# A gate projection by seven block products, with the residual brought back by feature tile

## The chip, the cores and the metric

The kernel runs on one core of one Trainium2 chip. The metric is the device time of that core in microseconds, the median of several runs. The profile shows one execution, with times in microseconds from the first instruction. Its engines are TensorE (PE; its weight loads apart as PEld), VectorE (DVE), ScalarE (ACT), GpSimd (POOL) and SyncE (SP), which here only issues DMAs.

## The reference

One decoder layer over 1024 tokens with 1024 features in float32. What the change touches is the last line, the gated per-layer input embedding; the half FFN before it (2816 hidden features) has the code that the change reuses:

```
x = x + 0.5 * swiglu(rms_norm(x, ffn2_norm), w_gate, w_up, w_down)
x = x + sigmoid(rms_norm(x, ple_norm) @ w_ple_gate) * (p @ w_ple_proj)
```

`w_ple_gate` is 1024 x 1024; `p @ w_ple_proj` is computed at the start of the kernel and lies in DRAM (`pd`, eight tiles of 128 features by 1024 tokens).

## The kernel before, in words

Activations lie with features on the 128 partitions and tokens along the columns, in two halves of 512 tokens. Every float32 operand is split into a high and a low part, and a product is three groups of matmuls: high by high, low by high, high by low. `split` (L112, L113) makes the parts: a cast on ScalarE, then a subtraction on VectorE.

The order of the instructions on each engine is written by hand: inside `tc.manual_schedule()` each engine runs its instructions in program order. Buffers come from rings by tag (`slot`; KH, Q, WL and others have 2 to 4 buffers each), and an instruction that writes a new tile waits until the last reader of the buffer's former tile is done. All DMAs are issued by SP, in program order.

`ffn` has an up pass and a down pass. The up pass takes groups of 256 features, gate and up weights in turn. Group 0 is done plainly (`plain`, L449): for two feature blocks and two token halves, 24 matmuls each. All other groups (numbered n) are seen as 2 x 2 blocks of features, times two token halves and two halves of the 1024 inputs, and are done by seven block products (m = 1 to 7, `product`, L496) of 12 matmuls each, where eight would be the plain count. The sums that this needs are made of the weights (`sums`, `last_sum`) and of the activations (the `combo_` functions); `evict` adds the products up in SBUF and in PSUM. `seqn` is the order of the (n, m), with s its index; `prep` splits the weight block of the product four places ahead (`LA`). The operands of the activations, B[1] to B[7], come from the tiles of the two halves: `combo_s` writes B[6] and B[7], `combo_d` and `combo_e` B[4].

The down pass (`make_down`; `product`, L388) also goes by seven products per chunk, each of them four tiles of 12 matmuls in its last chunk. It adds into the residual X in SBUF, two halves, and `last_norms` starts the next norm inside the last chunk. `second_entry` does the same for the projection before the second FFN: behind the output projection `oproj` (four k tiles) it stores X to DRAM (`xm`, L1570) in eight DMAs, loads the first weights, starts the plain group, and makes the sums. There the residual is loaded again later, since the up pass needs the buffers of X.

The last gate is done by `ple_steps` (L1644 to L1668): 16 units, one per feature tile and token half, of 24 matmuls each (the last in two parts of 256 columns). A unit ends with a sigmoid from PSUM on ScalarE (L1665), a multiply by the projection and an add of the residual, which is still in SBUF, on VectorE (L1666, L1667), and a store of 256 KB (L1668). `ple_start` puts the loads and splits of its weights, and the second half's norm (`second_half`), between the matmuls.

Of the kernel before, what the change touches and what calls it, by code (L numbers as in the profile page):

```python
# [18 lines left out]
P = 128  # L19
# [3 lines left out]
KD = D // P  # L23
# [15 lines left out]
def tile_hybrid_decoder_layer(  # L39
# [360 lines left out]
    def ffn(N, wg, wu, wd, next_gain, resid, hid, tags, entry, tail):  # L400

# [5 lines left out]
        wsrc = [kp(w[0]) for w in (wg, wu)]  # L407
        wdown = wd[0].rearrange("(j k p) n -> k p j n", k=2, p=P)
        LA = 4
        nm_ = 2 * NF  # L410
# [4 lines left out]
        seqn += [(n, 1), (n - 1, 4), (n, 2), (n, 6), (n, 5), (n, 7), (n - 1, 3), (n, 3), (n, 4)]  # L415
# [240 lines left out]
        manual[0] = True  # L656
        with tc.manual_schedule():
            entry(dict(m=combo_m, a=combo_a, t=combo_t, l=combo_l, u=combo_u, s=combo_s, load=load, prep=prep, sums=sums, last_sum=last_sum, plain=plain, silu=silu, product=product, evict=evict, norms=last_norms))
            for s, (n, m) in enumerate(seqn):
                evict(n, m, product(n, m))  # L660
                if s == 0:
                    for q in range(2):
                        combo_s(q, 7)
                elif s in (1, 5):
                    combo_d(s // 5)
                elif s in (6, 7):
                    combo_e(s - 6)
                if s + LA < len(seqn):
                    prep(*seqp[s + LA])
                if n % 2 and m == (4 if n == 1 else 3) and n < nm_ - 1:  # L670
                    hidden_sums(n, ("PT", "PT"))
                if s + LA < len(seqn):
                    if seqp[s + LA] == (nm_ - 2, 3):
                        down.wd_block(0, 0, 0, ("WH", "WH"))
                        down.load_hid(0, 0)
                if (n, m) == (nm_ - 1, 7):
                    down.wd_block(0, 1, 0, ("RAW", "RAW"))
                    down.load_hid(0, 1)
                    down.prep(0, 0)
                elif (n, m) == (nm_ - 1, 3):  # L680
                    down.wd_block(0, 0, 1, ("T", "T"))
                    down.wd_block(0, 1, 1, ("T", "T"))
            down.load_hid(0, 2)
            X = [slot("X", [P, KD, 512]) for _ in range(2)]

            def load_resid(half):
                for j in range(4):
                    nc.sync.dma_start(X[half][:, 2 * j:2 * j + 2, :], resid[half][:, 2 * j:2 * j + 2, :])

            load_resid(0)  # L690
            steps = [(c, i) for c in range(len(down.chunks)) for i in range(7)]
            for s, (c, i) in enumerate(steps):
                if s and s + 2 < len(steps):
                    down.load_hid(*steps[s + 2])
                final = c == len(down.chunks) - 1
                early = final and i == 3
                if s != 1 and s + 1 < len(steps):
                    down.prep(*steps[s + 1], *((1,),) * (final and i == 5))
                    if early:
                        down.after(*steps[s + 1])  # L700
                matmuls, evict_down = down.product(c, i, X)
                if s == 1:
                    load_resid(1)
                if s == 0:
                    for t in range(4):
                        matmuls(t)
                    down.wd_sums(0, 1)
                    down.wd_sums(0, 2)
                    hidden_sums(nm_ - 1, ("KH", "KL"))
                    down.prep(0, 2)  # L710
                    for t in range(4):
                        evict_down(t)
                    continue
                if final:
                    if i == 1:
                        nxt.extend(norm_begin(X[h], next_gain) for h in range(2))
                    for call in tail.get(i, ()):
                        call(X)
                for t in range(4):
                    matmuls(t, (lambda: (last_norms(5, 0.5, nxt), "late" in tail and down.prep(c, 6, (0,)))) if final and (i, t) == (5, 1) else None)  # L720
                    evict_down(t)
                    if final:
                        last_norms(i, t, nxt)
                        if (i, t) == (5, 0) and "late" not in tail:
                            down.prep(c, 6, (0,))
                        for call in tail.get((i, t), ()):
                            call(nxt)
                if s != 1 and s + 1 < len(steps) and not early:
                    down.after(*steps[s + 1])
            tail["end"](X, nxt)  # L730
        manual[0] = False
        return X, nxt
# [826 lines left out]
    def second_entry(F):  # L1559
# [12 lines left out]
        for i in range(7):  # L1572
# [52 lines left out]
    PLE_W = (NAT + ALT, (("WH", "WL"), ("T", "GF"), ("T", "RN"), ("PT", "PT")))  # L1625
    pl = {"w": {}, "raw": {}, "p": {}}

    def ple_load(d, qs):
        for q in qs:
            pl["raw"][d, q] = wraw_load([kp(w_ple_gate[0])[:, 2 * q:2 * q + 2, d * 512:d * 512 + 512]], 2, 512, ("Y", "RAW")[q // 2])  # L1630

    def ple_split(d, qs):
        for q in qs:
            pl["w"][d, q] = wsplit(pl["raw"].pop((d, q)), 2, 512, PLE_W[d][q])

    def ple_high(d, qs):
        for q in qs:
            pl["w"][d, q] = whigh(pl["raw"][d, q], 2, 512, PLE_W[d][q][0])

    def ple_low(d, q):  # L1640
        hi = pl["w"][d, q]
        pl["w"][d, q] = hi, wlow(pl["raw"].pop((d, q)), hi, 2, 512, PLE_W[d][q][1])

    def ple_p(v):  # L1644
        half, m = (v // 2) % 2, 4 * (v // 4) + 2 * (v % 2)
        r = pl["p"][v] = slot("KL", [P, 2, 512])
        nc.sync.dma_start(r[:], pd[m:m + 2, :, half * 512:half * 512 + 512].rearrange("m p n -> p m n"))

    def ple_steps(u):

        if u % 2 == 0 and u < 14:
            ple_p(u // 2 + 1)
        d, half, m = u // 8, (u // 4) % 2, u % 4
        o = slot(("Q", "KH")[u % 2], [P, 512])
        n = 2 if u == 15 else 1
        for j in range(n):
            cs = slice(j * 512 // n, (j + 1) * 512 // n)
            ps = ps1()[:, :512 // n]
            i = 0
            for a, b in ((0, 0), (1, 0), (0, 1)):  # L1660
                for k in range(KD):
                    pe(nc.tensor.matmul(ps, pl["w"][d, k // 2][b][:, k % 2, m * P:(m + 1) * P], hT[half][a][:, k, cs], start=(i == 0), stop=(i == 23)))  # L1662
                    i += 1
                    yield 0.216
            nc.scalar.activation(o[:, cs], ps, AF.Sigmoid)  # L1665
            nc.vector.tensor_mul(o[:, cs], o[:, cs], pl["p"][u // 2][:, u % 2, cs])  # L1666
            nc.vector.tensor_add(o[:, cs], o[:, cs], X[half][:, 4 * d + m, cs])  # L1667
            nc.sync.dma_start(out[half][:, 4 * d + m, cs], o[:, cs])  # L1668

    def ple_start():  # L1670
        def end(X_, N_):
            X.extend(X_)
            hT.extend(halves(N_))
            ple_p(0)
            side = second_half(N_[1], (28, 48, 7), ps2, ps2, ("PT", "PT", "PT", "Q"))
            side[100] = [lambda: ple_load(1, (0, 1))]
# [11 lines left out]
    for u in range(8, 16):  # L1688
        run(ple_steps(u))
# [36 lines left out]
```

## Time and profile before

| | before |
|---|---|
| median of 3 runs | 2233.55 us (2233.23 to 2233.89) |
| span of the profiled execution | 2230.9 us (no time around the span is recorded for it; the span is 2.6 us below the median) |
| TensorE, VectorE, ScalarE, GpSimd busy | 2218.2, 1490.2, 972.1, 813.9 us |
| DMA | 278.03 MB, 125 GB/s over the span |
| HBM read, written | 192.47 MB, 75.27 MB |

How to read it: busy is a sum over the span, in which the stages have different limits. Overlapping matmuls are shown longer than their pitch, so the pitch is read from the starts. The chain of waits follows the work that ended last back from its end; a timeline line gives start, duration, engine, line, operation, output and inputs, and in brackets the idle time ahead of it.

### The profile page before, as it was taken

What the parts mean: (1) busy time and instruction counts of PE and PEld (TensorE: products, weight loads), DVE (VectorE), ACT (ScalarE), POOL (GpSimd) and SP (SyncE); (2) the same over time, 40 slices, a digit from 0 to 9 for tenths busy, and PEclk for the clock granted to TensorE, in tenths of its full rate; (3) what the DMA queues carried; (4) which work ended last, traced back from release to release, by engine and by line L of the source; (5) the groups of instructions that cost most, each with busy time, mean ns of one, the idle gap of its engine ahead of it and who ended that gap; (6) DMA issues with size and microseconds to landing.
All of it is one profiled execution on the core that took longest, in us unless ns stands there. A gap on an engine that the chain in (4) does not pass through costs nothing.

```text
span 2230.9 us, 29212 instructions
## 1 busy us (share of the span) xinstructions
PE 2218.2 (99%) x10857; PEld 1864.3 (84%) x10857; DVE 1490.2 (67%) x2188; ACT 972.1 (44%) x1694; POOL 813.9 (36%) x709
## 2 busy tenths in 40 slices
PE   9999999999999999999999999999999999999999
PEld 7888888888889888888988888887888888888887
DVE  7855545497895565666666676799654555778873
ACT  6433333333454555555456564245333333434441
POOL 0344444310015466455456654400644443200111
PEclk9999999999999999999999999999999999999999
DMA  8232322474433133132124236731423232655132
GB/s 325 94 121 84 112 101 98 152 291 149 147 132 96 29 95 95 29 98 69 39 72 118 62 125 215 266 140 55 140 95 118 85 128 81 254 199 208 62 119 89
DMA packets 187710, 278.03 MB, mean 125 GB/s; under 512 B 27944, under 2 KB 110120, under 8 KB 187568
## 3 DMA queue, kind: packets, MB, share of 16 engines
q1 hardware_dynamic: 187568, 276.17, 36.7%
q8 instruction: 85, 1.39, 0.3%
q14 instruction: 57, 0.47, 0.1%
HBM read 192.47 MB, written 75.27 MB: 120 GB/s over the span
## 4 chain that ended last, share of the span: by engine, by line
PE 91%; DVE 4%; ACT 2%; issue 1%; DMA 1%; POOL 0%; SPq 0%; DVEq 0%; ACTq 0%; POOLq 0%
PE ps L496 36%; PE ps L388 19%; PE ps L763 11%; PE ps L755 7%; PE ps L1307 4%; PE ps L1662 4%; PE ps L1065 3%; PE ps L1042 2%; PE ps L449 2%; PE ps L991 1%; PE ps L990 1%; PE ps L1357 1%; DVE H L113 1%; ACT H L112 1%; ACT T L1001 0%
## 5 line engine op out<-in xcount | busy, mean ns | idle before, releaser
L388 PE MATMUL ps<-H,H 128*128 128x512 f32 x2184 | 497.3, 389 | 0.0
L388 PEld LDWEIGHTS ps<-H,H 128*128 128x128 f32 x2184 | 409.5, 188 | 85.0
L496 PE MATMUL ps<-H,WL 128*128 128x512 f32 x1008 | 238.9, 389 | 0.0
L496 PEld LDWEIGHTS ps<-H,WL 128*128 128x128 f32 x1008 | 189.2, 188 | 39.3
L763 PE MATMUL ps<-H,WH 128*128 128x512 f32 x640 | 176.1, 401 | 0.0
L1045 DVE TENSOR_TENSOR PT<-ps,PT 128x512 fp32r<-128x512 f32 (+1 forms) x160 | 100.6, 634 | 78.5 <-ACT PT L1044 77.6
L496 PE MATMUL ps<-H,Q 128*128 128x512 f32 x576 | 137.4, 389 | 0.0
L396 DVE SCALAR_TENSOR_TENSOR X<-ps,X 128x512 f32<-128x512 f32 x168 | 108.6, 682 | 41.8 <-PE ps L388 41.7
L763 PEld LDWEIGHTS ps<-H,WH 128*128 128x128 f32 x640 | 113.5, 188 | 18.4
L496 PEld LDWEIGHTS ps<-H,Q 128*128 128x128 f32 x576 | 108.1, 188 | 22.5
L1044 ACT CAST PT<-ps 128x512 fp32r<-128x512 f32 (+1 forms) x160 | 86.9, 549 | 85.0 <-PE ps L1042 81.1
L146 POOL TENSOR_TENSOR WL<-RAW,WH 128x512 fp32r<-128x512 f32 (+1 forms) x92 | 108.6, 1202 | 39.4 <-ACT WH L136 28.0
L496 PE MATMUL ps<-X,WL 128*128 128x512 f32 x480 | 115.6, 390 | 0.0
L209 POOL TENSOR_TENSOR PT<-PT,RN 128x1024 f32<-128x1024 f32 x2 | 4.8, 2413 | 295.0 <-ACT RN L203 295.0
L1065 PEld LDWEIGHTS ps<-PT,X 128*128 128x128 f32 x640 | 96.7, 189 | 18.9 <-DVE PT L1045 4.7
L755 PE MATMUL ps<-WH,H 128*128 128x256 f32 (+2 forms) x576 | 111.4, 323 | 0.2 <-DVE log_f L818 0.2
L1065 PE MATMUL ps<-PT,X 128*128 128x256 f32 (+1 forms) x640 | 105.7, 283 | 2.7 <-DVE PT L1045 1.4
L496 PEld LDWEIGHTS ps<-X,WL 128*128 128x128 f32 x480 | 89.9, 188 | 19.1 <-DVE WL L113 0.5
L1003 POOL TENSOR_TENSOR T<-T,l 128x128 f32<-128x128 f32 (+3 forms) x64 | 73.2, 1150 | 88.9 <-DVE l L1002 83.6
L496 PE MATMUL ps<-H,PT 128*128 128x512 f32 x432 | 103.2, 390 | 0.2 <-DVE PT L113 0.2
L283 POOL TENSOR_TENSOR PT<-GF,RN 128x512 f32<-128x512 f32 x20 | 33.2, 1658 | 174.1 <-DVE GF L539 89.9
L496 PEld LDWEIGHTS ps<-H,PT 128*128 128x128 f32 x432 | 80.8, 188 | 18.0 <-DVE PT L113 1.3
(418 smaller groups left out, 4810.8 us busy)
## 6 DMA issues: line engine op xcount, KB each, us to landing
hidden<-PT SPq DMA_DIRECT2D x40, 512.0 KB, 3.1
WH<-in_ffn_w_gate_dram SPq DMA_DIRECT2D x38, 512.0 KB, 5.4
Q<-hidden SPq DMA_DIRECT2D x24, 512.0 KB, 6.4
hidden<-RN SPq DMA_DIRECT2D x22, 512.0 KB, 2.6
KH<-in_ffn_w_up_dram SPq DMA_DIRECT2D x20, 512.0 KB, 6.2
KL<-in_ffn_w_up_dram SPq DMA_DIRECT2D x20, 512.0 KB, 6.9
T<-in_ffn_w_down_dram SPq DMA_DIRECT2D x20, 512.0 KB, 4.4
RAW<-in_w_in_dram SPq DMA_DIRECT2D x18, 512.0 KB, 4.3
```

The lines of the kernel that those rows point to most:

```text
L146: ins = eng_lo.tensor_sub(lo[part], raw[part], f(hi[part]))
L388: pe(nc.tensor.matmul(groups[g][t][:], wt[:, b, k, t * P:(t + 1) * P], act[:, a, k, :], start=(fresh and n == 0), stop=(i in (6, 1, 4) and ...
L396: nc.vector.scalar_tensor_tensor(xs, groups[g][t][:], scale, xs, ALU.mult, ALU.add)
L496: pe(nc.tensor.matmul(ps[:], hl[:, a, k, :], rhs(m, b, k), start=(first and i == 0), stop=(final and i == 11), skip_group_check=True))
L755: pe(nc.tensor.matmul(ps[:, :n], hT[t // 4][a][:, k, (t % 4) * P:(t % 4 + 1) * P], w[k // d][b][:, k % d, :n], start=(i == 0), stop=(i == ...
L763: pe(nc.tensor.matmul(ps[:], w[a][:, k, :], hT[half][b][:, k, :], start=(i == 0), stop=(i == 23)))
L1003: nc.gpsimd.tensor_mul(T[:, :n], T[:, :n], l[:].broadcast_to([P, n]))
L1044: high = nc.scalar.copy(pt[:, 0, :width], ps[:, :width])
L1045: low = nc.vector.tensor_sub(pt[:, 1, :width], ps[:, :width], f(pt[:, 0, :width]))
L1065: pe(nc.tensor.matmul(o, lh, r, start=(kpair == c and i == 0), stop=(kpair == 0 and i == 3)))
L1307: pe(nc.tensor.matmul(ps[:], w[a][:, k, :], yT[g][b][:, k, half * 512:half * 512 + 512], start=(i == 0), stop=(i == 11)))
L1662: pe(nc.tensor.matmul(ps, pl["w"][d, k // 2][b][:, k % 2, m * P:(m + 1) * P], hT[half][a][:, k, cs], start=(i == 0), stop=(i == 23)))
```

## The change

The up pass is cut out of `ffn` as `up_pass(N, wsrc, hid, tags, pairs)`, and the last gate runs through it with `pairs=False`: four groups of 256 features of `w_ple_gate`, the first plain, the other three by seven products, sigmoid in place of silu. It also takes the entry's code, cut out of `second_entry` as `after_products`. X cannot stay in SBUF there: it is stored to DRAM (`xo`) as its tiles are finished in the down pass, and comes back one feature tile of both halves at a time, beside the projection's tile (`fetch_px`). `complete` multiplies, adds and stores a feature tile, 512 KB. The tiles' two buffers of 512 KB are those of KH and Q in turn. The body of `ffn`, the products and the sums are the same as before, moved.

```
-            nc.scalar.activation(E[0][f_][:, half, :], bank_of.pop("plain")[:], AF.Silu)
+            nc.scalar.activation(E[0][f_][:, half, :], bank_of.pop("plain")[:], act)
...
+    def up_pass(N, wsrc, hid, tags, pairs=True):
...
-        nm_ = 2 * NF
+        nm_ = 2 * NF if pairs else 4
+        act = AF.Silu if pairs else AF.Sigmoid
...
+        if pairs:
+            seqn += [(n, 1), (n - 1, 4), (n, 2), (n, 6), (n, 5), (n, 7), (n - 1, 3), (n, 3), (n, 4)]
+        else:
+            seqn += [(n, 3), (n, 4)]
...
+        def last_product(n, m, parts=2):
+            ps, hl = bank_of[n, "b"], hls.pop((n, m))
+            for q in range(parts):
+                cs = slice(q * 512 // parts, (q + 1) * 512 // parts)
+                i = 0
+                for a, b in ((0, 0), (1, 0), (0, 1)):
+                    for k in range(4):
+                        pe(nc.tensor.matmul(ps[:, cs], hl[:, a, k, :], rhs(m, b, k)[:, cs], start=False, stop=(i == 11), skip_group_check=True))
+                        i += 1
+                yield cs, ps[:, cs]
...
+        def evict_gate(n, m, ps):
+            if m == 1:
+                E[n] = [slot(t, [P, 2, 512]) for t in (("Y", "Y") if n == 1 else ("GF", "RN"))]
+            e1, e2 = E[n]
+            to = {1: e1[:, 0, :], 2: e1[:, 0, :], 6: e1[:, 1, :], 3: e1[:, 1, :], 7: e2[:, 1, :], 4: e2[:, 0, :]}.get(m)
+            if m in (1, 6, 7):
+                nc.scalar.copy(to, ps[:])
+            if m in (2, 3, 7):
+                nc.vector.tensor_add(to, to, bank_of[n, "d"][:] if m == 7 else ps[:])
+            if m in (2, 3, 7):
+                nc.scalar.activation(to, to, act)
+            elif m == 4:
+                nc.scalar.activation(to, ps[:], act)
...
-    def ple_steps(u):
...
+    xo = dp.tile([2, P, KD, 512], F32, name="x_out")
+    by_tile = out.rearrange("h p k n -> p k h n")
...
+        def begin(X):
+            X_.extend(X)
+            return combo_begin(X[0], 3, True), combo_begin(X[1], 3, False)
+
+        def finished(half, j):
+            nc.sync.dma_start(xo[half][:, 2 * j:2 * j + 2, :], X_[half][:, 2 * j:2 * j + 2, :])
+
+        def fetch_px(m, tag):
+            px[m] = [slot(tag, [P, 2, 512]) for _ in range(2)]
+            nc.sync.dma_start(px[m][0][:], pd[m].rearrange("p (h n) -> p h n", h=2))
+            nc.sync.dma_start(px[m][1][:], xo[:, :, m, :].rearrange("h p n -> p h n"))
+
+        def complete(m, hs=slice(0, 2), cs=slice(0, 512)):
+            e = F["out"][m // 2][m % 2][:, hs, cs]
+            nc.vector.tensor_mul(e, e, px[m][0][:, hs, cs])
+            nc.vector.tensor_add(e, e, px[m][1][:, hs, cs])
+            nc.sync.dma_start(by_tile[:, m, hs, cs], e)
+
+        def end(X, N_):
+            after_products(F, N)
+            seqn, seqp, LA = F["seqn"], F["seqp"], F["ahead"]
+            for s, (n, m) in enumerate(seqn[:-1]):
+                F["evict"](n, m, F["product"](n, m))
+                if s == 0:
+                    for q in range(2):
+                        F["s"](q, 7)
+                elif s in (1, 5):
+                    F["d"](s // 5)
+                elif s in (6, 7):
+                    F["e"](s - 6)
+                if s + LA < len(seqn):
+                    F["prep"](*seqp[s + LA])
+                if s == 5:
+                    fetch_px(0, "KH")
+                elif s == 7:
+                    fetch_px(1, "Q")
+                elif 7 < s < 14:
+                    complete((0, 1, 2, 4, 3, 5)[s - 8])
+                    if s < 14:
+                        nx = (2, 4, 3, 5, 6, 7)[s - 8]
+                        fetch_px(nx, ("KH", "Q")[s % 2])
+                elif s == 14:
+                    complete(6, slice(0, 1))
+                    complete(7, slice(1, 2))
+                elif s == 15:
+                    complete(6, slice(1, 2))
+            for cs, ps in F["last_product"](*seqn[-1]):
+                nc.scalar.activation(F["out"][3][1][:, 0, cs], ps, AF.Sigmoid)
+                complete(7, slice(0, 1), cs)
+
+        hooks = {(i, t): [lambda N_, a=(i > 4, t // 2 + 2 * (i in (4, 5))): finished(*a)] for i in (1, 4, 5, 6) for t in (1, 3)}
+        hooks[5, 0] = [lambda N_: F["load"](0)]
+        hooks[6, 0] = [lambda N_: F["prep"](0, 1)]
+        hooks[6, 2] = [lambda N_: F["prep"](0, 2), lambda N_: F["load"](1)]
...
-    for u in range(8, 16):
-        run(ple_steps(u))
```

The planned order is (1,5) (2,5) (1,6) (2,6) (1,7) (2,7) (1,3) (2,3) (3,1) (3,2) (1,4) (2,4) (3,6) (3,5) (3,7) (3,3) (3,4), s = 0 to 16; the products (1,1) (1,2) (2,1) (2,2) come before it, in `products`.

More of the change, by code (lines that the diff above doesn't have):

```diff
@@ L400, in ffn @@
     def ffn(N, wg, wu, wd, next_gain, resid, hid, tags, entry, tail):
-        wsrc = [kp(w[0]) for w in (wg, wu)]
+        F = up_pass(N, [kp(w[0]) for w in (wg, wu)], hid, tags)
+        load, prep, product, evict, hidden_sums = F["load"], F["prep"], F["product"], F["evict"], F["hidden_sums"]
+        combo_s, combo_d, combo_e, last_norms = F["s"], F["d"], F["e"], F["norms"]
+        seqn, seqp, nm_, LA = F["seqn"], F["seqp"], F["n"], F["ahead"]
         wdown = wd[0].rearrange("(j k p) n -> k p j n", k=2, p=P)
+        down = make_down(wdown, hid, [(0, 4), (4, 7), (7, 11)], 0.5, ("Y", "PT"))
@@ L506, in right @@
             return t[:, b, k, :]
+        def evict_gate(n, m, ps):
[11 more added lines that the diff above has]
+                nc.scalar.activation(to, ps[:], act)
         def evict(n, m, ps):
             up, j = n % 2, n // 2
+            if not pairs:
+                return evict_gate(n, m, ps)
             if m == 1:
@@ L654, in last_norms @@
                     fold(b, 1)
[L656 to L730, printed above, removed]
@@ L731, in ffn @@
-        manual[0] = False
-        return X, nxt
+        return dict(m=combo_m, a=combo_a, t=combo_t, l=combo_l, u=combo_u, s=combo_s, d=combo_d, e=combo_e, load=load, prep=prep, sums=sums, last_sum=last_sum, plain=plain, silu=silu, product=product, last_product=last_product, evict=evict, out=E, hidden_sums=hidden_sums, norms=last_norms, seqn=seqn, seqp=seqp, n=nm_, ahead=LA)
     def wload_nat(w, cols, tags=(("WH", "WL"), ("WH", "WL")), eng_lo=nc.gpsimd):
@@ L1604, in second_entry, with after_products @@
                 oproj.after(0, i + 1)
+        after_products(F, N)
+    def after_products(F, N):
         F["plain"](0, 0, (0,))
@@ L1623, in second_entry @@
         products(F)
[L1625 to L1647, printed above, removed]
-    def ple_steps(u):
[L1651 to L1676, printed above, removed]
-            side[124] = [lambda: ple_load(1, (2, 3))]
-            for i in range(4):
-                side[148 + 11 * i] = [lambda i=i: ple_split(1, (i,))]
-            weave(seq(*[ple_steps(u) for u in range(8)]), side)
-        return {3: [lambda X: ple_load(0, (0, 1))], 4: [lambda X: ple_split(0, (0, 1))], 5: [lambda X: ple_load(0, (2, 3))], (5, 2): [lambda N: ple_high(0, (2, 3))],
-                (5, 3): [lambda N: ple_low(0, 2), lambda N: ple_low(0, 3)], "late": True, "end": end}
+    xo = dp.tile([2, P, KD, 512], F32, name="x_out")
@@ new lines, in tile_hybrid_decoder_layer, with gate_start @@
+    by_tile = out.rearrange("h p k n -> p k h n")
+    def gate_start():
+        N = []
+        tags = {"raw": {0: ("RAW", "RAW"), 1: ("WH", "WH"), 2: ("RAW", "RAW"), 3: ("WH", "WH")}, "sum": {1: "WH", 2: "KL", 3: "KL"}, "w": ("Q", "Q", "KH", "KH"), "hl": ("WL", "WL", "WL", "KL") + ("PT",) * 6 + ("WL", "WL", "PT", "WL", "WL", "PT", "WL", "WL", "WL", "PT", "WL", "PT", "WL", "PT", "WL")}
+        F = up_pass(N, [kp(w_ple_gate[0])], None, tags, False)
+        X_, px = [], {}
+        def begin(X):
[13 more added lines that the diff above has]
+        def end(X, N_):
+            after_products(F, N)
+            seqn, seqp, LA = F["seqn"], F["seqp"], F["ahead"]
+            for s, (n, m) in enumerate(seqn[:-1]):
+                F["evict"](n, m, F["product"](n, m))
+                if s == 0:
+                    for q in range(2):
+                        F["s"](q, 7)
+                elif s in (1, 5):
+                    F["d"](s // 5)
+                elif s in (6, 7):
+                    F["e"](s - 6)
+                if s + LA < len(seqn):
+                    F["prep"](*seqp[s + LA])
[20 more added lines that the diff above has]
+        hooks[6, 2] = [lambda N_: F["prep"](0, 2), lambda N_: F["load"](1)]
+        return {**hooks, "late": True, "begin": begin, "norms": N, "tags": ((("PT", "RN", "GF", "RN"), ("GF", "RN", "KH", "KL"), ("GF", "RN", "WH", "PT")),), "end": end}
```

80 lines of the change are left out of this document (74 added, 6 removed).

## The prediction

> **What bounds the kernel now.** I read the page's engine line first, then the chain of waits that ended last, then the stages one by one.
>
> ```profile
> span 2230.9 us, 29212 instructions
> PE 2218.2 (99%) x10857; PEld 1864.3 (84%) x10857; DVE 1490.2 (67%) x2188; ACT 972.1 (44%) x1694; POOL 813.9 (36%) x709
> ```
> ```profile
> 2150.20 76.53 PE ps L1662 x360
> ...
> 2226.75 0.39 ACT KH L1665
> ...
> 2227.17 0.44 DVE KH L1666
> ...
> 2227.63 0.42 DVE KH L1667
> ```
> ```profile
> 1550.00:1560.00 10.00, 10.00 (x45) 8.02 (x44) 9.89 (x13) 4.31 (x7) 0.00 (x0) 1.00 0.16 52
> ...
> 2160.00:2180.00 20.00, 20.00 (x89) 16.54 (x89) 8.69 (x11) 6.43 (x9) 6.23 (x5) 1.00 0.63 211
> 2180.00:2227.00 47.00, 46.72 (x229) 39.49 (x227) 14.11 (x19) 5.42 (x10) 5.39 (x4) 1.00 0.26 87
> ```
>
> TensorE sets the end: it works 99% of the span, and the last gate (L1662) is an unbroken chain of matmuls. Behind its last matmul come a sigmoid, a multiply, an add and a store: VectorE ends at 2227.63 + 0.42 = 2228.05, 1.3 us behind TensorE, and the span ends 2.9 us later. In the windows (columns: time, TensorE, weight loads, VectorE, ScalarE, GpSimd, clock, DMA share, GB/s) the gate leaves VectorE mostly idle: 14.1 of the last 47 us. The first line is from the second up pass, whose code the new gate takes over: there VectorE works 9.89 us of 10. The change moves the gate from a stage where TensorE alone is short of time to one where VectorE is too. The clock is 1.00 in all three.
>
> **Part 1, the products.** Columns here: start, us, engine, line, count.
>
> ```profile
> 1488.10 13.88 PE L388 MATMUL ps<-H,H 128*128 128x512 f32 x60
> 1501.82 2.88 PE L449 MATMUL ps<-H,WL 128*128 128x512 f32 x12
> ...
> 1537.39 5.60 PE L496 MATMUL ps<-H,PT 128*128 128x512 f32 x24
> ...
> 1570.21 2.88 PE L496 MATMUL ps<-H,WL 128*128 128x512 f32 x12
> 1572.93 2.88 PE L496 MATMUL ps<-H,Q 128*128 128x512 f32 x12
> ...
> 2123.24 13.90 PE L388 MATMUL ps<-H,H 128*128 128x512 f32 x60
> 2136.97 1.07 PE L1662 MATMUL ps<-H,WH 128*128 128x512 f32 x4
> ...
> 2139.23 0.73 PE L1662 MATMUL ps<-H,T 128*128 128x512 f32 x2 [0.73 <-ACT H L270]
> ```
>
> A product of 12 matmuls takes 1572.93 - 1570.21 = 2.72 us, so 0.227 us per matmul. The old gate has 16 x 24 = 384 matmuls; the new one 96 for group 0 and 3 x 84 = 252 for the others: 36 fewer, 8.2 us. The new gate runs the entry of the second up pass behind a down chunk of the same size (four k tiles), with the same norm calls, so I price its start by that entry: from the down pass's end (1488.10 + 13.88 = 1501.98) to the first product in the planned order, (1,5) at 1537.39, are 35.4 us, transposes and short waits included. There follow 17 products x 2.72 = 46.2 us: TensorE could end at 1583.63 on this clock, 81.7 us behind the down pass. The old gate takes 2226.73 - 2137.14 = 89.6 us (down pass's end: 2123.24 + 13.90). On TensorE alone the change gains 7.9 us; splitting the last product in two costs 0.25 of it, as 48 matmuls of 256 columns took 5.9 us before where 24 of 512 take 5.4. Removed with the old gate are its weight splits on ScalarE and GpSimd and VectorE's normalisation of the second half, all hidden under its matmuls: no gain. The eight stores of the residual leave at steps where the second entry has eight stores of the same size; nothing in that entry waits for them, so I cost them at nothing.
>
> **Part 2, VectorE up to the first finished tile.** The steps s = 0 to 7 of the planned order have the products of the up pass; their VectorE work can be read there.
>
> ```profile
> 1553.67 0.69 DVE L534 TENSOR_TENSOR RN<-RN,Y 128x512 f32<-128x512 f32 x1
> ...
> 1554.88 0.68 DVE L519 TENSOR_TENSOR RN<-RN,ps 128x512 f32<-128x512 f32 x1
> ...
> 1557.87 0.68 DVE L113 TENSOR_TENSOR WL<-WH,WL 128x512 fp32r<-128x512 f32 x1
> 1558.47 0.68 DVE L523 TENSOR_TENSOR Y<-Y,ps 128x512 f32<-128x512 f32 x1
> 1559.19 1.23 DVE L539 TENSOR_TENSOR GF<-GF,Y 128x1024 f32<-128x1024 f32 x1
> 1560.33 1.22 DVE L113 TENSOR_TENSOR X<-Q,X 128x1024 fp32r<-128x1024 f32 x1
> 1561.47 0.68 DVE L113 TENSOR_TENSOR WL<-WH,WL 128x512 fp32r<-128x512 f32 x1
> 1562.07 0.68 DVE L523 TENSOR_TENSOR GF<-GF,ps 128x512 f32<-128x512 f32 x1
> 1564.81 1.23 DVE L113 TENSOR_TENSOR X<-Q,X 128x1024 fp32r<-128x1024 f32 x1 [2.06 <-ACT X L112]
> ...
> 1566.56 0.68 DVE L462 TENSOR_TENSOR KL<-WH 128x512 f32<-128x512 f32 x1
> ...
> 1568.00 0.69 DVE L464 TENSOR_TENSOR KL<-WH 128x512 f32<-128x512 f32 x1
> 1569.44 1.24 DVE L113 TENSOR_TENSOR WL<-KL,WL 128x512 fp32r<-128x512 f32 x1 [0.74 <-ACT WL L112]
> ```
> ```profile
> 1563.75 1.03 ACT L112 CAST X<-Q 128x1024 fp32r<-128x1024 f32 x1
> ```
> ```profile
> L1665 ACT ACTIVATE Q<-ps 128x512 f32<-128x512 f32 x8 | 4.8, 598 | 27.2 <-PE ps L1662 27.2
> ```
>
> By the starts, 512 columns cost VectorE 0.60 us and 1024 cost 1.14 (1560.33, 1561.47, 1562.07). Out go the two gate-times-up products (L534, L539; 1.7 us). In comes a sigmoid of 0.6 behind (1,3), ahead of the cast (1.03) for B[4] on ScalarE's queue, so both subtractions of that split wait as the second does now (2.06). Written out: low part of (3,1) done 1557.3; add of (1,3) 1557.9; sigmoid 1558.5; cast 1559.5; subtraction 1560.7; low of (3,2) 1561.3; add of (2,3) 1561.9; sigmoid and cast 1563.6; subtraction 1564.8; low of (2,4) 1565.4. Then s = 8: three weight sums at 0.72, the wait of 0.74 and 0.6 for the low part of (3,6): 1568.9. The first complete is a multiply and an add, 2 x 1.14: done at 1571.2, while its product ended at 1537.39 + 9 x 2.72 = 1561.9. VectorE is 9.3 us late there. At s = 9: add 0.6, sigmoid and cast on ScalarE (1.2), low 0.6, complete 2.3: 1575.9. Steps 10 to 12 cost 0.6 + 2.3 = 2.9 each against TensorE's 2.72: the delay is never worked off.
>
> **Part 3, the fetches.** Each tile completed stores 512 KB and lets the next fetch of 2 x 512 KB (projection, residual) take its two buffers, KH or Q in turn. On SP's queue the store stands ahead of the two loads and waits for the add, so they wait too. Two chains result, tiles 0, 2, 3, 6 and 1, 4, 5, 7, each one fetch deep. The trace before has no such chain; its rows bound the cost.
>
> ```profile
> 5.00:30.00 25.00, 23.81 (x109) 19.46 (x108) 17.98 (x27) 20.67 (x38) 2.04 (x2) 1.00 1.03 402
> ```
> ```profile
> L1647 SPq DMA_DIRECT2D KL<-p_proj x8: 360/378/1040, 2141.3 to 2206.0; - x8
> ...
> DMA to landing us min/median/max: 3.8/4.4/4.8
> ```
> ```profile
> Q<-hidden SPq DMA_DIRECT2D x24, 512.0 KB, 6.4
> ...
> GF<-hidden SPq DMA_DIRECT2D x14, 512.0 KB, 9.0
> ```
> ```profile
> 2008.21 0.93 SPq L338 DMA_DIRECT2D Q<-hidden  x2
> 2009.19 0.94 SPq L309 DMA_DIRECT2D WH<-in_ffn_w_down_dram  x2
> 2010.18 0.98 SPq L309 DMA_DIRECT2D RAW<-in_ffn_w_down_dram  x2
> 2011.20 0.49 SPq L338 DMA_DIRECT2D GF<-hidden  x1
> ```
>
> With the DMA engines full (share 1.03) they move 402 GB/s: a store and two loads are 1.57 MB, 3.91 us. A tile of TensorE's work is 2.72. A lone 512 KB load lands in 3.8 us at best, 1.3 of it data: 2.5 fixed. So a tile's data land 2.5 us after its add's release or when the engines are through with the group before, whichever is later, plus 3.91. Run from the two adds at 1571.2 and 1575.9:
>
> tile 2 lands 1577.6, added 1578.8 (its multiply waits for the low part of (3,7) first); tile 4 lands 1582.4, added 1583.5; tile 3 lands 1586.3, added 1587.4; tile 5 1590.2, 1591.3; tile 6 1594.1; tile 7 1598.0, its first half added 1598.6.
>
> Behind that stand, on VectorE's queue, the add of (3,3) 0.6, its sigmoid 0.75 with the handover, the second half of tile 6, 1.2, and four operations on 256 columns for the last block, 1.85 in all (the chain above: 0.44 + 0.42 for two, with starts 0.46 apart): 1603.0. With the 2.9 us of the last store as before, the span ends at 1605.9, 103.9 us behind the down pass, where it was 2230.9 - 2137.14 = 93.8. **Sum: +10.2 us.** TensorE itself stalls about 3 us ((3,4)'s low part stands behind tile 4's add), but ends 16 us ahead of VectorE, so the stall costs nothing more.
>
> Both ends of this cost. With every landing in time, VectorE's own work from 1575.9 (2.9 x 3 + 2.3 + 3.0 + 2.55 + 1.85 us) ends at 1594.3: +1.4. With the loads of a crowded queue, 9.0 us, each round is 0.8 to issue + 9.0 + 1.14 and tile 7 lands at 1575.9 + 2 x 10.9 + 9.8 = 1607.6: +19.8. With 6.4 it is +12.0. I take the chain at 402 GB/s: like the pair loads at 6.4 it has few transfers in flight, while the 9.0 row's loads leave SP in a burst behind six others (2008 to 2011).
>
> Two rules of the Trainium skill put other prices on this term. Its page "DMA: Bandwidth & Descriptors", section "Where 436 GB/s comes from", says that between HBM and SBUF the HBM side binds at about 358 GB/s; a group is then 4.39 us, an estimate that moves the sum to +12.6. The trace's 402 with one core running speaks against it. Section "Anatomy of one DMA" of the same page gives 2.0 us plus bytes at 436 GB/s: 3.2 us for 512 KB, against 3.8 in the row; the sum by it is +8.2. Either way the sign stays.
>
> **The rivals.**
>
> A, the forecast: the two fetch chains and VectorE's backlog set the end, 2243.7.
>
> B, no change: the fetches are early enough and VectorE alone sets the end, +1.4: 2235.0. For it: tiles 0 and 1 are fetched early, into free engines (share 0.16 in the window 1550 to 1560). Against: 3.91 us of data per tile against 2.9 of VectorE.
>
> C, faster: VectorE's delay at s = 8 disappears and the matmuls set the end again, -7.6: 2225.9. It decides only if VectorE ends less than 4.5 us behind TensorE (1.3 now); B leaves 10.4, so about 6 us of the 9.3 at the first complete would have to be wrong, and the data in time as well. For it: GpSimd, whose work lengthens VectorE's in the up pass (the low parts at 1569.44 take 1.24 instead of 0.68), has almost none in the gate. Against: the window 1550 to 1560 above has GpSimd at 0.00 already.
>
> D, worse: loads land as late as in the down pass (9.0), 2253.4. Against: no other loads are due.
>
> **How the numbers follow.** The profiled span of 2230.9 is 2.6 below the median of the runs, 2233.55; I add the change to the median, since the work around the span stays. Chances: A 0.72, B 0.14, C 0.05, D 0.09. Forecast 2233.55 + 10.2 = 2243.7; A's own range is 2241 (the faster price) to 2247. The range 2234 to 2248 holds A and B and leaves out C and D. A change of 0.2% is 4.5 us, about what can be told from none: slower (above 2238.0) is D and nearly all of A, 0.79; same is B and a little of A, 0.16; faster 0.05.
>
> **What would show it.** Right: the chain of waits ends in VectorE's complete lines and DMA, not matmuls; TensorE ends over 10 us before the span does; the DMA share in the last 30 us is near 1; VectorE waits for px loads. The step of the products is right if a product takes 2.72 us and the gate's first planned product starts some 35 us behind the down pass. Wrong: VectorE at (3,1) less than 5 us late, or loads that land in under 5 us in pairs with the store, or TensorE's own stalls in the entry of more than 3 us.

## The result, and the profile after

The changed kernel takes 2249.77 us (median of 5 runs, 2248.74 to 2251.96), the kernel before 2233.53 in the same comparison. The ratio is 1.0074 (95% interval 1.0062 to 1.0086): slower by 16.2 us. The forecast was 2243.7 with a range up to 2248, which the result leaves by 1.8 us.

The profiled execution of the changed kernel, page:

```profile
span 2248.0 us, 29192 instructions
PE 2216.3 (99%) x10809; PEld 1859.2 (83%) x10809; DVE 1533.1 (68%) x2242; ACT 988.0 (44%) x1718; POOL 787.7 (35%) x694
```

TensorE has 48 matmuls and 1.9 us less, VectorE 43 us more. The shares hardly move (99 and 68%), so they don't tell what happened; the end of the chain of waits does (start, us, engine and what):

```profile
2215.53 6.54 DMA Q<-x_out
...
2222.17 1.24 DVE GF L1690
...
2224.41 5.81 DMA Q<-x_out
...
2230.31 1.24 DVE RN L1690
...
2232.59 6.96 DMA Q<-x_out
...
2239.65 0.69 DVE RN L1690
2240.34 0.61 DVE GF L616
2240.97 0.63 ACT GF L618
2241.60 0.28 ACT RN L1722
2241.92 1.95 PE ps L596 x12
...
2244.77 0.42 DVE RN L1690
```

Where the chain of before was 76 us of unbroken matmuls, this one is three rounds of the buffers of tag Q: load of the residual, add (L1690), store, next load. TensorE's timeline of the same execution:

```profile
2124.13 13.88 PE L388 MATMUL ps<-H,H 128*128 128x512 f32 x60
...
2173.40 5.60 PE L585 MATMUL ps<-H,PT 128*128 128x512 f32 x24
...
2184.28 2.88 PE L585 MATMUL ps<-X,PT 128*128 128x512 f32 x12
2187.00 3.04 PE L585 MATMUL ps<-X,WL 128*128 128x512 f32 x12
...
2215.95 2.90 PE L585 MATMUL ps<-X,WL 128*128 128x512 f32 x12
2232.19 4.95 PE L585 MATMUL ps<-T,PT 128*128 128x512 f32 x12 [13.33 <-DVE RN L616]
...
2241.92 1.94 PE L596 MATMUL ps<-X,WL 128*128 128x256 f32 x12 [3.36 <-ACT RN L1722]
```

The down pass ends at 2124.13 + 13.88 = 2138.01. From there to the end of the span are 110.0 us; before it was 93.8, and the forecast said 103.9. Below I call this stretch the gate and use it beside the medians, since the end of the down pass lay anywhere from 2137.06 to 2138.21 in the traces of the changed kernels below, whose code is the same up to there but for the place where e7 and e9 store the residual. The gate's first planned product starts at 2173.40, 35.4 us behind the down pass. Fifteen of the seventeen products are through by 2218.85. Then TensorE stands for 13.33 us, until VectorE has reached the add of (3,7).

VectorE's timeline in the same stretch, with the idle time ahead and who ended it in brackets:

```profile
2190.85 0.69 DVE L113 TENSOR_TENSOR WL<-RAW,WL 128x512 fp32r<-128x512 f32 x1 [1.21 <-ACT WL L112]
...
2206.06 1.22 DVE L113 TENSOR_TENSOR WL<-KL,WL 128x512 fp32r<-128x512 f32 x1 [0.74 <-ACT WL L112]
2207.20 1.21 DVE L1689 TENSOR_TENSOR GF<-GF,KH 128x1024 f32<-128x1024 f32 x1
2208.45 1.22 DVE L1690 TENSOR_TENSOR GF<-GF,KH 128x1024 f32<-128x1024 f32 x1
...
2213.33 1.23 DVE L1690 TENSOR_TENSOR RN<-RN,Q 128x1024 f32<-128x1024 f32 x1
...
2220.76 1.23 DVE L1689 TENSOR_TENSOR GF<-GF,Q 128x1024 f32<-128x1024 f32 x1 [2.59 <-DMA Q<-p_proj]
...
2228.96 1.23 DVE L1689 TENSOR_TENSOR RN<-RN,Q 128x1024 f32<-128x1024 f32 x1 [1.70 <-DMA Q<-p_proj]
...
2238.40 0.69 DVE L1689 TENSOR_TENSOR RN<-RN,Q 128x512 f32<-128x512 f32 x1 [3.58 <-DMA Q<-p_proj]
```

Until 2214 VectorE's waits are for ScalarE's casts; from 2220 to 2240 they are for loads. The windows of the same execution (columns: TensorE, weight loads, VectorE, ScalarE, GpSimd, clock, DMA share, GB/s):

```profile
2209.00:2240.00 31.00, 14.31 (x51) 10.87 (x49) 18.86 (x21) 5.37 (x10) 0.00 (x0) 0.72 0.90 313
2215.00:2220.00 5.00, 3.86 (x15) 2.79 (x14) 3.12 (x4) 0.58 (x1) 0.00 (x0) 0.91 0.93 290
2220.00:2225.00 5.00, 0.00 (x0) 0.00 (x0) 3.35 (x4) 0.00 (x0) 0.00 (x0) 0.77 1.02 399
2225.00:2230.00 5.00, 0.00 (x0) 0.00 (x0) 3.19 (x3) 0.00 (x0) 0.00 (x0) 0.50 1.01 348
2230.00:2235.00 5.00, 2.81 (x7) 2.23 (x8) 3.39 (x5) 0.63 (x1) 0.00 (x0) 0.50 1.02 355
2235.00:2240.00 5.00, 3.56 (x19) 2.92 (x17) 1.04 (x2) 0.00 (x0) 0.00 (x0) 0.86 0.75 254
```

No compute engine is full there: TensorE works 14.3 of 31 us and VectorE 18.9. The DMA engines are full from 2220 to 2235, and their bytes per second at the same share differ: 348 to 399. Ahead of that and behind it they move less, 290 and 254.

### The profile page after: what moved, and what is told of

The parts are those of the page before. It is cut to its first block, busy times and chain, and to the rows that moved or that the text cites. A ratio compares the mean times of both kernels' runs of the same rounds, so it can differ in the third digit from the quotient of the medians.

```text
span 2248.0 us, 29192 instructions
## 1 busy us (share of the span) xinstructions
PE 2216.3 (99%) x10809; PEld 1859.2 (83%) x10809; DVE 1533.1 (68%) x2242; ACT 988.0 (44%) x1718; POOL 787.7 (35%) x694
## 4 chain that ended last, share of the span: by engine, by line
PE 90%; DVE 5%; ACT 2%; DMA 2%; issue 1%; POOL 0%; SPq 0%; DVEq 0%; ACTq 0%; POOLq 0%
PE ps L585 36%; PE ps L388 20%; PE ps L800 11%; PE ps L792 7%; PE ps L1344 4%; PE ps L1102 3%; PE ps L1079 2%; PE ps L538 2%; PE ps L1028 1%; PE ps L1027 1%; PE ps L1394 1%; DMA Q<-x_out 1%; ACT H L112 0%; DMA RAW<-in_w_in_dram 0%; DVE RN L1003 0%
## 5 line engine op out<-in xcount | busy, mean ns | idle before, releaser
L585 PE MATMUL ps<-H,WL 128*128 128x512 f32 x1068 | 253.3, 389 | 0.1
L585 PEld LDWEIGHTS ps<-H,WL 128*128 128x128 f32 x1068 | 200.4, 188 | 42.1 <-DVE WL L113 0.5
L585 PE MATMUL ps<-H,PT 128*128 128x512 f32 x516 | 125.2, 395 | 2.3 <-ACT PT L112 1.9
L585 PE MATMUL ps<-X,WL 128*128 128x512 f32 x504 | 121.5, 390 | 0.0
L585 PEld LDWEIGHTS ps<-H,PT 128*128 128x128 f32 x516 | 97.3, 190 | 25.2 <-DVE PT L113 2.6
L585 PEld LDWEIGHTS ps<-X,WL 128*128 128x128 f32 x504 | 94.5, 188 | 20.3 <-DVE WL L113 0.8
L1102 PE MATMUL ps<-PT,X 128*128 128x256 f32 (+1 forms) x640 | 105.9, 283 | 2.8 <-DVE PT L1082 1.5
L1050 POOL TENSOR_TENSOR T<-T,RN 128x383 f32<-128x383 f32 (+2 forms) x64 | 77.3, 1209 | 48.2 <-DVE RN L1003 45.9
```

The lines of the kernel that those rows point to most:

```text
L585: pe(nc.tensor.matmul(ps[:], hl[:, a, k, :], rhs(m, b, k), start=(first and i == 0), stop=(final and i == 11), skip_group_check=True))
L1050: nc.gpsimd.tensor_mul(T[:, cut:n - 1], T[:, cut:n - 1], R[:, cut:n - 1])
L1102: pe(nc.tensor.matmul(o, lh, r, start=(kpair == c and i == 0), stop=(kpair == 0 and i == 3)))
```

## The experiments

All kernels of one comparison ran on the same chip beside the kernel before; the ratio is to that one, with its 95% interval. There were four comparisons below, and the kernel before had medians of 2233.04 to 2233.78 in them, so a difference between kernels of different comparisons is good to about 0.7 us. "Gate" is the span minus the end of the down pass, from each trace.

| kernel | median us | ratio | gate us |
|---|---|---|---|
| before | 2233.5 | 1 | 93.8 |
| after | 2249.77 | 1.0074 (1.0062 to 1.0086) | 110.0 |
| e4_bare | 2227.53 | 0.9975 (0.9965 to 0.9985) | 88.2 |
| e1_no_fetch | 2240.70 | 1.0034 (1.0021 to 1.0047) | 101.2 |
| e2_deep | 2240.86 | 1.0034 (1.0021 to 1.0047) | 101.0 |
| e3_late_sigmoid | 2244.18 | 1.0050 (1.0033 to 1.0067) | 104.7 |
| e5_deep_late | 2235.54 | 1.0010 (1.0001 to 1.0020) | 95.6 |
| e6_reorder | 2233.27 | 1.0000 (0.9990 to 1.0010) | 93.8 |
| e8_one_load | 2244.96 | 1.0053 (1.0038 to 1.0068) | 105.9 |
| e10_swap | 2245.96 | 1.0055 (1.0040 to 1.0071) | 106.8 |
| e7_accum | 2235.15 | 1.0009 (1.0000 to 1.0019) | 95.9 |
| e9_mixed | 2234.23 | 1.0002 (0.9993 to 1.0011) | 94.8 |
| e11_filled | 2232.99 | 0.9997 (0.9988 to 1.0006) | 93.1 |

### The products alone: e4_bare

```
 def complete(m, hs, cs):
-    nc.vector.tensor_mul(e, e, px[m][0][:, hs, cs])
-    nc.vector.tensor_add(e, e, px[m][1][:, hs, cs])
     nc.sync.dma_start(by_tile[:, m, hs, cs], e)
...
-    all fetch_px(...)
```

> No fetches and no multiply and add in the completes; the sigmoid is stored as it is. What is left is the products alone. By the prediction's price of the products (17 products of 2.72 us behind the entry, sigmoid and store) the span would be 7.6 us less than before if VectorE kept up; with VectorE's late low parts at steps 3 to 9 and the wait of the last half product for a sigmoid about 2 us of that are lost: 2226 to 2228. If the entry or the products themselves were mis-priced: above 2230.

Measured: 2227.53, 5.7 us faster than the kernel before in the same comparison, 2233.21 (5.6 in the gate). Its TensorE timeline:

```profile
2215.52 3.02 PE L585 MATMUL ps<-T,PT 128*128 128x512 f32 x12 [1.40 <-DVE RN L616]
...
2220.44 1.69 PE L596 MATMUL ps<-X,WL 128*128 128x256 f32 x12 [0.47 <-ACT RN L1713]
```

The 36 matmuls saved are real time, less some 2 us of waits: 1.40 for the add of (3,7), which has to read (3,5) from a PSUM bank before (3,3) is added to it there, and 0.47 for the read of the last product's first half. Whatever completes the tiles must cost less than 6 us on the path for the change to gain.

### The fetches: e1_no_fetch and e2_deep

e1 leaves out the fetches of tiles 2 to 7; e2 keeps every byte, but issues them early, into the free buffers of tags H and RAW and the first of KH:

```
 e1:  -  fetch_px(nx, ("KH", "Q")[s % 2])
      +  px[nx] = px[s % 2]
 e2:  +  s == 8:  fetch_four(2, 4)     # one tile of tag H, [P, 4, 2, 512]
      +           complete(0)
      +  s == 9:  fetch_four(3, 5); fetch_px(6, "RAW"); fetch_px(7, "KH")
      +           complete(1)
```

> Tiles 2 to 7 are multiplied and added with the data of tiles 0 and 1, so only two of the eight tiles are fetched; every other instruction stays, the stores too. Fetch theory (beyond VectorE's own work, the end is set by the rounds of store and fetch, 7 to 8 us each in the trace of the changed kernel): no wait for data is left, VectorE runs from the first complete's end at 2209.7 through 2.4 us per tile and the low parts to about 2234, span 2237, time 2239 (11 us less than the changed kernel, 5 to 6 over the kernel before). Backlog theory (VectorE's lateness at the first complete and its own work set the end, the fetches only fill its gaps): 2247 to 2250.

> The same bytes as the changed kernel, but tiles 2 to 5 are fetched into the two large H buffers that products (3,1) and (3,2) free, tile 6 into RAW, tile 7 into KH, all of them ahead of the stores on SP's queue but tile 7. If the depth of the fetches is what costs (each waits for an add two tiles back): as without fetches, about 2239. If the DMA engines' rate is what costs, whatever the order (8 MB of loads and 4 MB of stores at 350 to 400 GB/s are 31 to 36 us): the loads end by about 2217 since they start 12 us earlier, so the gain is nearly the same but some waits stay, 2240 to 2243. Backlog theory: 2247 to 2250.

Measured: 2240.70 and 2240.86, 9 us under after and level with each other. The same window of e1, then of e2:

```profile
2205.00:2225.00 20.00, 9.58 (x41) 7.12 (x39) 18.35 (x18) 4.95 (x10) 0.93 (x1) 0.87 0.35 132
```
```profile
2205.00:2225.00 20.00, 9.55 (x41) 7.11 (x39) 18.38 (x18) 4.92 (x10) 0.89 (x1) 0.86 1.02 381
```

With 132 GB/s or with 381, VectorE does the same work in the same time. So the bytes cost nothing once they are asked for early enough, and no contention of the transfers with VectorE shows; the 9 us come from loads that had to wait for the add and the store two tiles ahead. Inside that chain the bytes do count, as e8 shows below. What is left in e2, its VectorE and TensorE timelines show:

```profile
2223.88 1.23 DVE L1697 TENSOR_TENSOR RN<-RN,H 128x1024 f32<-128x1024 f32 x1
2225.02 0.68 DVE L616 TENSOR_TENSOR RN<-RN,ps 128x512 f32<-128x512 f32 x1
...
2230.53 0.69 DVE L616 TENSOR_TENSOR GF<-GF,ps 128x512 f32<-128x512 f32 x1 [2.17 <-PE ps L585]
```
```profile
2225.76 4.74 PE L585 MATMUL ps<-T,PT 128*128 128x512 f32 x12 [9.28 <-DVE RN L616]
```

No wait for data is left. But the add of (3,7) stands behind six completed tiles on VectorE's queue; (3,3) on TensorE waits 9.28 us for it, and VectorE then waits 2.17 for (3,3). The two engines wait for each other in turn.

### The sigmoids: e3_late_sigmoid and e5_deep_late

```
 evict_gate:
-    if m in (2, 3, 7):
+    if m in (3, 7) and n == 3:
         nc.scalar.activation(to, to, act)
 end():  + behind prep at s = 9 to 12, the same sigmoids, in place
```

> The sigmoids of groups 1 and 2 (and of product (3,2)) go behind the weight casts of steps 9 to 12 on ScalarE's queue, as one of 1024 columns where two were of 512; VectorE's waits for casts of 1.2, 1.6, 1.6 and 1.2 us at steps 3, 6, 7 and 9 should go. Both theories: the first complete ends about 4 us earlier. Fetch theory: every round of fetches starts that much earlier, time 2245 to 2246. If the fetch rounds were tied to something that does not move (the buffers, TensorE), it stays at 2249 to 2250.

> The deep fetch and the late sigmoids together. With all data in time VectorE still waited 1.2, 1.6, 1.6 and 1.2 us for casts (trace of the deep fetch), 5.7 in all; if VectorE's chain alone sets the end there, all of it comes off: 2240.9 - 5.7 = 2235.2. If the late sigmoids helped in their own run only by starting the fetches earlier, nothing comes off here: 2240 to 2241.

Measured: e3 5.6 us under after; e5 (e3's edit on e2) 5.3 under e2. In e3 VectorE's first finished tile:

```profile
2203.80 1.23 DVE L1690 TENSOR_TENSOR GF<-GF,KH 128x1024 f32<-128x1024 f32 x1
```

From the end of the down pass (2137.60 here) it ends 67.4 us later, in after 71.7: the sigmoid that waits for VectorE's add, and the cast behind it that VectorE's next subtraction waits for, cost 4.2 us there. By the gate e3 gains 5.3; the other 1.1 were not followed.

### The order of the completes: e6_reorder and e11_filled

On e5, e6 puts tile 3 behind the add of (3,7), and tiles 5, 6 and 7 behind that of (3,3); e11 puts both 3 and 5 between the two adds.

```
 e6:   s == 14: complete(3)
       s == 15: complete(5); complete(6); complete(7, slice(1, 2))
 e11:  s == 14: complete(3); complete(5)
       s == 15: complete(7, slice(1, 2)); complete(6)
```

> As the deep fetch with late sigmoids, but tiles 3, 5, 6 and 7 are completed behind the add of product (3,7), so that (3,3), which waits for that add (9.3 us in the deep fetch's trace), starts earlier and VectorE no longer waits for it (2.2 us) near the end. If VectorE's work is the bound, its last waits go: 2232.5 to 2233.5, level with the kernel before. If something else holds the end (the last product's halves, the stores), 2235 as without the reorder.

> From the reorder (deep fetch, late sigmoids, level with the kernel before): tile 5 is completed between the adds of (3,7) and (3,3) too, which fills VectorE's last wait of 2.0 us, and the half of tile 7 that is ready goes ahead of tile 6. If VectorE's work is all that is left, the span falls by 1.5 to 2 us to about 2229: 2231.2 to 2231.8, 0.1% under the kernel before. If the last product's halves, now a step later behind the add and the sigmoid of (3,3), set the end instead: 2232.5 to 2233.5.

Measured: e6 2233.27, 2.3 us under e5 (1.7 by the gate) and level with before; e11 2232.99, level too. e6's VectorE timeline shows what the order left:

```profile
2219.66 0.69 DVE L616 TENSOR_TENSOR GF<-GF,ps 128x512 f32<-128x512 f32 x1 [1.99 <-PE ps L585]
...
2227.63 0.42 DVE L1697 TENSOR_TENSOR RN<-RN,KH 128x256 f32<-128x256 f32 x1
```

e11 fills that wait of 1.99 (some 1.3 of it goes with the clock: (3,3) took 4.29 us in e6's trace and 3.02 in e11's), and VectorE is done at 2226.42 + 0.42 = 2226.84, 88.9 us behind its down pass (e6: 91.0). But its span ends 4.2 us behind VectorE, where e6's ends 2.9 behind. e11's window, and the landing of the last stores in e11 and in e6 (KB each, median us):

```profile
2224.00:2226.00 2.00, 0.43 (x3) 0.14 (x1) 1.94 (x4) 0.38 (x1) 0.00 (x0) 0.50 1.05 408
```
```profile
out_dram<-RN SPq DMA_DIRECT2D x2, 128.0 KB, 3.3
```
```profile
out_dram<-RN SPq DMA_DIRECT2D x2, 128.0 KB, 1.7
```

Now the last stores queue in full DMA engines: 3.3 us to land in place of 1.7. Of VectorE's gain of 2.1 us the transfers give back 1.3.

### What a fetch round is made of: e8_one_load and e10_swap

e8 fetches the projection only; e10 keeps both loads, ahead of the store on SP's queue.

```
 e8:   -  nc.sync.dma_start(px[m][1][:], xo[:, :, m, :]...)
       -  nc.vector.tensor_add(e, e, px[m][1][:, hs, cs])
       +  nc.vector.tensor_add(e, e, px[m][0][:, hs, cs])
 e10:  complete(m, store=False); fetch_px(nx, tag); put(m)
```

> The changed kernel with the residual's load left out of each fetch (the add takes the projection's tile a second time): order, depth, stores and VectorE's work stay, the bytes of a round go from 1.57 to 1.05 MB, 3.91 to 2.61 us at 402 GB/s. If the bytes set the rounds (engines full, one tile per 3.9 to 4.4 us), they fall under VectorE's 2.9 us per tile and the time falls nearly to that without fetches, 2240 to 2242. If the depth sets them (add, store's and load's issue 0.9, a landing of 4.4, multiply and add 2.5: 7.8 us per round of two tiles, where the changed kernel shows 8.2 to 8.8), it falls by 2 to 3 us only: 2246 to 2248.

> The changed kernel with each fetch issued ahead of the store of the tile that frees its buffers, instead of behind it. The bytes stay. If the depth of the fetch sets the rounds, each round is shorter by the store's issue (0.4 us) and its 512 KB (1.3 us), over three rounds 4 to 5 us: 2245 to 2246. If the bytes set them (the engines never idle between 2210 and 2240), only the last fetch gains, by one store: 1.5 to 2 us, 2248.

Measured: e8 4.8 us under after (4.1 by the gate), between the two values that the theories had given; e10 3.8 under it (3.2 by the gate), at 2245.96, within the 2245 to 2246 of the depth theory. e8's VectorE timeline:

```profile
2220.12 1.22 DVE L1688 TENSOR_TENSOR GF<-GF,Q 128x1024 f32<-128x1024 f32 x1 [1.87 <-DMA Q<-p_proj]
...
2227.35 1.23 DVE L1688 TENSOR_TENSOR RN<-RN,Q 128x1024 f32<-128x1024 f32 x1 [1.52 <-DMA Q<-p_proj]
...
2234.83 0.69 DVE L1688 TENSOR_TENSOR RN<-RN,Q 128x512 f32<-128x512 f32 x1 [3.07 <-DMA Q<-p_proj]
```

With half the bytes to load, VectorE still waits 6.5 us at these three places (7.9 in after). So both matter: the loads' bytes and the fixed way round (release, issue, landing). From the end of an add in the Q chain to the landing of the loads it releases, e8 takes 5.4, 4.7 and 4.9 us, at DMA shares of 0.84, 0.77 and 0.77. The prediction's own price for a round of 1.05 MB is 2.5 + 2.61 = 5.1, so it holds where the engines aren't full.

In e10 the same stretches take 5.6, 6.6 and 6.8 us. The last two in its windows:

```profile
2221.26:2227.87 6.61, 0.00 (x0) 0.00 (x0) 4.26 (x4) 0.00 (x0) 0.00 (x0) 0.59 1.03 402
2229.17:2236.00 6.83, 5.79 (x24) 4.74 (x24) 2.67 (x4) 0.63 (x1) 0.00 (x0) 0.74 1.03 405
```

Two things changed for e10's loads. They no longer stand behind the store's 512 KB; and the projection's load, whose buffer is free as soon as the multiply has read it, now leaves SP 1.3 to 2.0 us ahead of the residual's (2213.07 against 2214.33 in the first round), where in after it stood behind the store and so behind the add. The run doesn't divide its 3.8 us between the two. How much of the 9 us is bytes and how much is the way round, e8 and e10 don't divide exactly either.

### Saving the residual's way back: e7_accum and e9_mixed

On e6, the residual goes to `out` itself and the product is added by the DMA; in e9 for tiles 0, 1, 2 and 4 only. e9 also completes tile 3 two steps and tile 5 one step earlier than e6, and the half of tile 7 ahead of tile 6.

```
 -  nc.vector.tensor_add(e, e, px[m][1][:, hs, cs])
 -  nc.sync.dma_start(by_tile[:, m, hs, cs], e)
 +  nc.gpsimd.dma_start(by_tile[:, m, hs, cs], e, accum_op=ALU.add)
```

> As the reorder, but the residual is stored to the output itself in the down pass and the completed tile (sigmoid times projection) is added to it by an accumulating DMA from GpSimd's queue: eight adds of 1.2 us leave VectorE, and the loads of the residual leave the DMA engines. If VectorE's work is the bound, the products become it again: span near the bare kernel's 2225.3 plus 2 to 4 us for the slower last store, time 2228 to 2231. If an accumulating DMA of 512 KB is much slower than a plain store (over 8 us each), the last of them ends later: 2236 or more.

> From the reorder: tiles 0, 1, 2 and 4 get their residual by an accumulating DMA (no residual load, no add on VectorE for them), tiles 3, 5, 6 and 7 as before; the residual is stored to the output in the down pass and loaded from there. VectorE loses four adds of 1.2 us, and the accumulating DMAs (8 us to landing, about 200 GB/s in the run with all tiles) are issued by 2211 and done by 2220, ahead of the last plain stores. If VectorE's work is what is left, the span ends near 2228, 2 to 3 us under the kernel before: 2230.3 to 2231.3. If the slow accumulating DMAs hold up the loads and stores that share the engines with them, 2233 or more.

Measured: 2235.15 and 2234.23, neither under before. e7's queues from 2195 to 2240 (packets, MB, share of 16 engines; then KB each and median us to landing), and a window:

```profile
q0 software_dynamic: 2336, 4.19, 57.0%
...
out_dram<-GF POOLq DMA_DIRECT2D x3, 512.0 KB, 7.8
...
out_dram<-RN POOLq DMA_DIRECT2D x2, 128.0 KB, 8.2
```
```profile
2206.00:2224.00 18.00, 14.71 (x74) 11.98 (x72) 10.96 (x14) 7.18 (x13) 7.37 (x8) 1.00 1.03 189
```

VectorE is relieved (10.96 us of 18), but the accumulating DMAs fill the engines at 189 GB/s, and the last ones, of 128 KB each, take 8.2 us to land: VectorE is done at 2223.45, and the span ends at 2233.9. In e9 the plain loads beside them are late, as its queues and its VectorE timeline show (the same load took 9.8 us in e6):

```profile
KH<-out_dram SPq DMA_DIRECT2D x1, 512.0 KB, 19.3
```
```profile
2224.74 0.69 DVE L1700 TENSOR_TENSOR RN<-RN,KH 128x512 f32<-128x512 f32 x1 [3.30 <-DMA KH<-out_dram]
```

No version is clearly under the kernel before. e6 and e11 are level with it, and the bare products, with nothing done to complete them, are only 5.6 us of gate under it.

## Why the prediction was right or wrong

The direction and the mechanism were right: the chain ends in complete's lines and DMA, VectorE waits for px loads, the DMA share is near 1. The size was off: the span grew by 17.1 us where the sum was 10.2. The steps that failed are the rate of the DMA engines in Part 3, the wait for casts in Part 2, and TensorE's stall, which was put at nothing. Of the 6.9 us between, 0.9 lie ahead of the gate (the down pass ended at 2138.01, in the execution of before at 2137.14), no more than the traces of the changed kernels differ there. The rest, by steps:

**Part 1, right.** The first planned product comes 35.4 us behind the down pass, as priced, and a product takes 2.72 (2187.00 - 2184.28). e4 shows the gain by itself: 5.6 us of the 7.6 forecast, the rest being the two waits above (1.87).

**Part 2, mis-sized by 2.6 us.** On the clock of before (shifted by 2138.01 - 1501.98 = 636.03) the first finished tile was due at 1571.2. Its add ended at 2208.45 + 1.22 = 2209.67, which is 1573.6. Three terms make this up. The row at 2190.85 shows a wait of 1.21 for a cast that a sigmoid had delayed; such a sigmoid was counted behind (1,3) and (2,3), but not behind (1,7), where it is the same code. The low part of (3,6) took 1.14 by the starts (2206.06, 2207.20) and was priced at 0.6, though the row at 1569.44, quoted in the prediction, gave 1.24 for it. GpSimd was at work beside it (2205.45 to 2206.73), as in the up pass, so the point that spoke for rival C did not come. And at (3,1) the start of a row was read as its end, 0.6. Sum 2.3. The second tile was then 2.6 late, which is what Part 3 starts from. e3 shows the size of the whole effect: 4.2 us at the first tile for the sigmoids' place.

**Part 3, mis-sized by 2.9 us.** From the end of an add in the Q chain to the landing of the loads that it releases, the trace has 7.5, 6.8 and 8.0 us (2214.56 to 2222.07, 2223.41 to 2230.22, 2231.55 to 2239.55); the forecast had 6.5, 6.7 and 6.7. That is 2.4, and the multiply and add behind a landing another 0.5. The term that failed is the 402 GB/s. It came from the start of the kernel before; here the engines moved 329, 359 and 298 GB/s in these three stretches, at shares of 0.97, 1.01 and 0.89 (in the last 1.5 us of the third they were no longer full). In the prediction's own chain the 336 of all 25 us put the last landing 3.8 later, the 367 of 2220 to 2235 put it 1.8 later, and the miss of 2.9 lies between. e10's two rounds at 402 and 405 take 6.6 and 6.8, as forecast, though its loads also leave earlier. So the rate accounts for the miss within what these rows allow; no run changed the rate alone. The Trainium skill's page "DMA: Bandwidth & Descriptors", section "Where 436 GB/s comes from", has the HBM side bind at about 358 GB/s; the sum by it, +12.6, lay nearer to the +16.2 measured. The 399 of the window 2220 to 2225, and 408 in e11, lie above that figure, so it is no fixed limit for one core either. The other rule of the Trainium skill that was weighed (the same page, section "Anatomy of one DMA", 2.0 us plus bytes at 436 GB/s, which the page fits to DMAs issued by GpSimd, while these are SP's; +8.2) was farther off.

**The tail, 0.6 us.** From the last landing to VectorE's end 5.0 was forecast, and 5.6 was taken (2239.55 to 2244.77 + 0.42). The two halves of the last product share a PSUM bank, and the second half waited for ScalarE's read of the first (3.36 us on TensorE); the prediction had all matmuls done by then.

With the 0.9 these are 0.9 + 2.6 + 2.9 + 0.6 = 7.0, the 6.9 within rounding.

**The rivals.** B (the data in time, VectorE alone, +1.4) was mis-sized by more than A: e1 is this case, and costs +7.5. Its 6 us too little are 2.6 from Part 2, 2.4 for the wait for (3,3) (2.17 in e2's row), and some 1 us of tail and of steps that take 3.0 us in place of 2.9. That the fetches then add 9 us, near the 10.2 - 1.4 = 8.8 of the forecast, is luck: both ends came out 6 us short, in part by different terms. The dependency was missed: (3,3) adds to the bank that the add of (3,7) reads, and that add stands behind the completes. So the claim that TensorE "ends 16 us ahead of VectorE, so the stall costs nothing more" was wrong: TensorE stood for 13.33 us and ended at 2243.86, 1.3 us ahead of VectorE and 4 us ahead of the span, not over 10. In after this was covered by the loads; in e1 and e2 it was on the path. C (faster) needed VectorE within 4.5 us of TensorE: even e6, with fetches, sigmoids and order mended, only reaches the time of before. D (9.0 us per load) did not come: the gate's loads take 5.0 (projection) and 5.7 us (residual) to land in the median, and 7.4 at most.

**How the 16 us divide.** By the medians, with the gates within 0.6 us of them, 9 us are the fetch rounds (after against e2), 5.3 the sigmoids ahead of the casts (e2 against e5), 2.3 the order on VectorE's queue (e5 against e6); each was removed on top of the one before. What is then left, 5.7 us over the bare products (e6 against e4), cancels the matmuls saved.

## What to carry to other kernels

Where a buffer is freed by an add, its store and the next load follow on one queue, and the next add waits for that load, the round of release, issue and landing sets the pace; free buffers to start all loads early gave back 9 us here without saving a byte. When an operation is put between others on an in-order engine (a sigmoid on ScalarE), follow the next instruction of that queue to whoever waits for it, at every place where the same code runs and not only at the one in view. And before an engine's stall is costed at nothing, look up which PSUM bank its next write needs, and where the reader of that bank stands in its own queue.

## What the runs showed of the hardware

DMA engines with a share of 1.01 to 1.05 moved 348, 355, 399 (after), 381 (e2, over 20 us) and 408 GB/s (e11) with plain loads and stores mixed, and 189 with accumulating DMAs (e7). In e10, where the loads stand ahead of the store, two rounds moved 402 and 405. A full share is thus no measure of the bytes. Why plain transfers differ by a sixth was not tried.

When TensorE stands, its granted clock can fall. It idled from 2218.85 in after, and the windows above have 0.77 for 2220 to 2225 and 0.50 from 2225; the 12 matmuls of (3,3), right behind, took 4.95 us, where 2.88 to 3.04 is the rule at a clock of 1.00. In e2 the same 12 took 4.74, and there VectorE waited for them: by an estimate 4.74 - 2.88 = 1.9 us of the path come from the clock, which no run separates. A short stand can be enough: in after TensorE stood 1.92 us ahead of (3,5), the clock was 0.50 from 2213 to 2215, and that product took 4.62; in e6 (3,3) took 4.29 behind 1.78 us. But (3,5) in e2 took 3.02 behind 1.93, and (3,3) in e11 3.02 behind 1.76. So one trace doesn't tell what a stand of 2 us will cost. The Trainium skill's page "TensorE: Matmul & The Clock Gate", section "What's actually happening", states a half clock after an idle window of about 3.4 us; the two long stands are of that kind, while the short ones show that TensorE need not idle that long.
